# Output projection to up stage of a hybrid encoder layer: last row's scaling and third pair's weights ahead of casts, rows in two pools, four casts behind the block sums

## The chip, the cores and the metric

The kernel runs on one core of one Trainium2 chip. The metric is the time of one execution in device microseconds; the time of before is the median of three runs. The engines are TensorE (PE, with its weight loads PEld), VectorE (DVE), ScalarE (ACT), GpSimd (POOL) and SyncE (SP), which issues DMAs. Each takes its instructions in order, and they wait for each other through semaphores.

## The reference

One encoder layer over 1024 tokens (and 16 meta tokens) of width 1024. Cut to the part around the change:

```python
mix = jax.nn.sigmoid(gate_na) * y_na + jax.nn.sigmoid(gate_hg) * y_hg
h = h + mix @ w_o[l]                                   # output projection
m = rms_norm(h, norm_mlp[l])                           # each row scaled by rsqrt(mean(h*h) + eps), times a gain
h = h + jnp.square(jax.nn.relu(m @ w_up[l])) @ w_down[l]
```

Before it stand the input projection, a neighbourhood attention and a gated linear recurrence; behind it a final RMSNorm. All is float32.

## The kernel before

Every float32 matrix product is made of three matmuls: each operand is split into a rounded part (hi, cast by ScalarE) and the rest (lo, subtracted by VectorE), and hi*hi, hi*lo and lo*hi are added in PSUM. A split is thus one ScalarE cast and one VectorE subtraction of a 128x512 block.

**Output projection** (wo_rows). Eight rows of 128 tokens, two column halves each, 24 matmuls a half, into five PSUM banks in turn. VectorE adds each half into hres[i], into which SP has loaded that row of x. Then row_scale stores the row to DRAM (hsp[i], needed at the end of the layer), ScalarE squares it and sums, GpSimd makes the factor rs, and scale_row (VectorE) multiplies the row in place. TensorE transposes the scaled row in 128x128 blocks (turn_back), and row_sums makes the combinations of blocks that a Strassen-Winograd product needs: t1, t2, t3, t4 from b11, b21, b12, b22. Row j and row j+4 go together, so j runs from 0 to 3. split_rows casts one variant of one j into hi and lo tiles (nT, mT, nt1, nt3, nt4).

**Up stage.** w_up is worked off in 16 pairs of 128 columns. Each pair has seven products of 12 matmuls (chain, lines 918 to 920): product 1 with b11, 2 with b21, 3 with b22, 6 with t2, 5 with t1, 7 with t3, 4 with t4. Its weights are block sums (winograd, lines 908 to 911, four VectorE additions) and raw blocks, each split by weights (lines 1328 and 1329: tiles wh and wl). Pairs 0, 1 and 2 are early: their products 1 and 2 need no block sums, and run first, straight after the last row of the output projection, with weights loaded by first_load (tile sx). Then a loop takes pair 0's products 3, 6, 5, 7, and for the next pairs the rest, with the block sums of the next pair made by VectorE meanwhile.

**What sets the order.** From first_load(2) on, the order on TensorE, ScalarE, VectorE and GpSimd is as the code writes it (manual_schedule). The list todo holds the variants still to be cast: nine of j = 0 to 2 (t1, t3, t4), and five of j = 3. splits() takes the next ones; product_1 and product_2 call it between groups of three matmuls. Row 7 is finished in there: its square, its scaling (L1243), its transposes (L1268) inside pair 1's product 1, and row_sums(3) (VectorE L1249 and L1250, GpSimd L1251 and L1252).

**Memory.** The eight hres rows stand in one pool. When it closes, two loads of w_up for whole pairs (tile raw, L1355) and a second set of weight tiles (pool upr) take their place; each load waits for the last reader of the rows that it covers.

Of the kernel before, what the change touches and what calls it, by code (L numbers as in the profile page):

```python
# [9 lines left out]
F32 = mybir.dt.float32  # L10
F32R = mybir.dt.float32r
# [37 lines left out]
def layer(ctx: ExitStack, tc: tile.TileContext, x, meta, w_in, w_na, w_hg, w_o, w_up, w_dn,  # L49
# [1150 lines left out]
    hress = ExitStack()  # L1200
    hrp = hress.enter_context(tc.tile_pool(name="hrp", bufs=1, side="right", reuse_waits="tile"))
    hres = [None] * 8
    for i in (2, 6, 3, 7, 0, 4, 1, 5):
        hres[i] = hrp.tile([P, D], F32, name=f"hres{i}")
# [26 lines left out]
    def row_scale(i):  # L1231

        ssq = rowp.tile([P, 1], F32, tag="ssq", name="ssq", bufs=4)
        rs = rowp.tile([P, 1], F32, tag="rs", name="rs", bufs=4)
        tm = rowp.tile([P, 1], F32, tag="rtm", name="rtm", bufs=4)
        junk = rowp.tile([P, D], F32, tag="junk", name="junk", bufs=2)
        act.dma_start(hsp[i], hres[i])
        act.activation(junk, hres[i], AF.Square, accum_out=ssq)
        rsqrt_mean(rs, ssq, D, tm)
        return rs  # L1240
# [4 lines left out]
    def row_sums(j):  # L1245

        b11, b21, b12, b22 = (hres[i][:, q:q + TH] for i in (j, j + 4) for q in (0, TH))
        t2 = rowp.tile([P, TH], F32, tag="t2", name="t2", bufs=3)
        dve.tensor_tensor(b11, b12, b11, op=ALU.subtract)  # L1249
        dve.tensor_tensor(t2, b22, b11, op=ALU.subtract)  # L1250
        pool.tensor_tensor(b12, b22, b12, op=ALU.subtract)  # L1251
        pool.tensor_tensor(b21, b21, t2, op=ALU.subtract)  # L1252
        return {"t1": b11, "b22": b22, "t3": b12, "t2": t2, "t4": b21}
# [69 lines left out]
    def weights(src, pool_=None):  # L1323
        if pool_ is None:
            w_pools.append(w_pools.pop(0))
        hi, lo = (a_tile(pool_ or w_pools[-1], t, F32R, 1 if pool_ else 4) for t in ("wh", "wl"))
        v = (lambda t: t.rearrange("p (k c) -> p k c", c=P)) if len(src.shape) == 3 else (lambda t: t)
        act.copy(v(hi), src)  # L1328
        dve.tensor_tensor(v(lo), src, v(hi).bitcast(F32), op=ALU.subtract)  # L1329
        return hi, lo  # L1330
# [122 lines left out]
    def last_first_weights(k):  # L1453
        if k == 2:
            first_w[2].append(weights(first_raw[2][:, 4:], upf))

# [5 lines left out]
    with tc.manual_schedule(engines={e.engine for e in (pe, act, dve, pool, sp)}):  # L1462

        rs7 = row_scale(7)
        todo = [(v, j) for j in range(3) for v in ("t1", "t3", "t4")]
        todo += [(v, 3) for v in ("b22", "t2", "t1", "t3", "t4")]
# [5 lines left out]
        def last_row(k):  # L1472
            if k == 0:
                scale_row(7, rs7)
            elif k == 3:
                turn_back(hres[7][:, :TH], dve)
                turn_back(hres[7][:, TH:], act)
                nB.append(row_sums(3))
            else:
                splits()  # L1480

        product_1(pairs[0], first_w[0][0], lambda k: splits(k > 0))
        product_1(pairs[1], first_w[1][0], last_row)
        first_weights(2, 0)
        splits(2)
        product_1(pairs[2], first_w[2][0], lambda k: splits(), "mm")
        product_2(pairs[0], first_w[0][1], lambda k: (splits(k < 3), last_first_weights(k)))
# [4 lines left out]
        upr = ups.enter_context(tc.tile_pool(name="upr", bufs=1, side="right", reuse_waits="tile"))  # L1492
# [4 lines left out]
        next_weights(-1, "s4", "s2")  # L1497
        product_2(pairs[2], first_w[2][1])
# [3 lines left out]
        w_pools.insert(0, upr)  # L1502
        next_weights(-1, "s1", "s3", "a22")
        for m, q in enumerate(pairs):
# [3 lines left out]
            if m == 0:  # L1508
                product_6(q)
            if m + 1 < NP:  # L1510
                pair_sums(pairs[m + 1])
# [41 lines left out]
    ups.close()  # L1553
    up_s.close()
# [311 lines left out]
```

## Time and profile before

| | us |
|---|---|
| median of 3 runs | 1512.63 (1512.05 to 1513.26) |
| profiled execution | 1511.24 |
| its span, first to last instruction | 1509.5 |
| TensorE busy | 1492.1 |
| VectorE busy | 1035.8 |
| ScalarE busy | 665.0 |
| GpSimd busy | 370.7 |

The output projection runs from about 797 to 886 us of the span, products 1 and 2 of the early pairs from 885.7 to 907.4, the loop of the up stage to about 1197, and the down projection from there to the end. In rows of the trace the first number is the start in us from the start of the span, the second the duration; then come engine, line, operation, output and inputs, shapes, count, and in brackets the idle time before it and what ended that.

### The profile page before, as it was taken

To read this page: it belongs to the slowest core of one execution; us is meant where nothing else is said; L and a number is where in the kernel's file an instruction comes from. 1 tells how busy PE (TensorE), PEld (TensorE's weight loads), DVE (VectorE), ACT (ScalarE), POOL (GpSimd) and SP (SyncE) were. 2 spreads that over 40 slices of the span, in tenths; PEclk is the share of its full clock that TensorE was granted. 3 is DMA by queue.
4 is the path that set the end of the run, shared out by engine and by line. 5 is a ranking of instruction groups with operands and counts; after the bars stand their busy time and mean duration, and the time that the engine had idled before them with its cause. 6 is when DMAs were issued, how large, how long until landed. Compare 5 with 4: busy or idle time off the path is not lost.

```text
span 1509.5 us, 23492 instructions
## 1 busy us (share of the span) xinstructions
PE 1492.1 (99%) x9200; PEld 1250.8 (83%) x9200; DVE 1035.8 (69%) x1622; ACT 665.0 (44%) x1185; POOL 370.7 (25%) x349
## 2 busy tenths in 40 slices
PE   9999999999999999999999999999999999999998
PEld 8888888888888888888888878888888888888886
DVE  7876666656786796675585478777777445877876
ACT  7131313135565576343133355555555534334444
POOL 3313131324414400110000131344444200231242
PEclk9999999999999999999999999999999999999999
DMA  4211011114212237444655124544444676563224
GB/s 170 59 30 57 29 50 37 44 30 132 87 63 95 98 91 259 140 152 168 223 169 209 42 91 167 168 154 154 154 154 153 203 252 234 189 233 112 96 84 154
DMA packets 142592, 195.62 MB, mean 130 GB/s; under 512 B 8192, under 2 KB 90368, under 8 KB 142480
## 3 DMA queue, kind: packets, MB, share of 16 engines
q1 hardware_dynamic: 133072, 172.34, 34.8%
q10 hardware_dynamic: 7232, 14.44, 2.5%
q0 software_dynamic: 2176, 7.34, 1.3%
q8 instruction: 72, 1.18, 0.3%
q14 instruction: 40, 0.33, 0.1%
HBM read 139.56 MB, written 54.53 MB: 129 GB/s over the span
## 4 chain that ended last, share of the span: by engine, by line
PE 92%; DVE 4%; issue 2%; ACT 2%; POOL 0%; DMA 0%; POOLq 0%; ACTq 0%; DVEq 0%
PE mm L122 11%; PE mm L123 11%; PE mm L124 11%; PE mm L1541 5%; PE pa L1541 5%; PE pb L918 4%; PE pb L919 4%; PE pb L920 4%; PE pb L1541 4%; PE pc L1541 4%; PE pc L920 3%; PE pc L919 3%; PE pc L918 3%; PE pa L920 2%; PE pa L919 2%
## 5 line engine op out<-in xcount | busy, mean ns | idle before, releaser
L122 PE MATMUL mm<-aT,hi 128*128 128x512 f32 (+2 forms) x600 | 213.9, 357 | 0.0
L123 PE MATMUL mm<-aT,hi 128*128 128x512 f32 (+2 forms) x600 | 211.9, 353 | 0.0
L124 PE MATMUL mm<-aT,lo 128*128 128x512 f32 (+2 forms) x600 | 211.7, 353 | 0.0
L96 ACT CAST dh<-ur 128x1024 fp32r<-128x1024 f32 x54 | 56.9, 1054 | 166.5 <-issue 91.1
L97 DVE TENSOR_TENSOR dl<-ur,dh 128x1024 fp32r<-128x1024 f32 x54 | 70.0, 1297 | 87.0 <-ACT dh L96 85.2
L122 PEld LDWEIGHTS mm<-aT,hi 128*128 128x128 f32 x600 | 113.2, 189 | 12.6
L124 PEld LDWEIGHTS mm<-aT,lo 128*128 128x128 f32 x600 | 113.2, 189 | 12.3
L123 PEld LDWEIGHTS mm<-aT,hi 128*128 128x128 f32 x600 | 113.3, 189 | 12.0
L1333 ACT ACTIVATE uv<-uv 128x512 f32<-128x512 f32 x48 | 30.4, 633 | 82.3 <-DVE uv L1441 52.8
L1329 DVE TENSOR_TENSOR wl<-sx,wh 128x512 fp32r<-128x512 f32 x70 | 62.1, 897 | 3.6 <-ACT wh L1328 3.6
L1329 DVE TENSOR_TENSOR wl<-raw,wh 128x512 fp32r<-128x512 f32 x50 | 39.0, 783 | 36.4 <-ACT wh L1328 36.3
L112 ACT CAST hi<-raw 128x1024 fp32r<-128x1024 f32 x26 | 27.3, 1052 | 77.1 <-PE mm L123 71.3
L1328 ACT CAST wh<-sx 128x512 fp32r<-128x512 f32 x70 | 42.3, 620 | 38.5 <-PE pc L919 24.8
L1631 POOL TENSOR_TENSOR w<-w,tt 128x512 f32<-128x512 f32 x16 | 24.3, 1521 | 132.3 <-DVE tt L1630 111.1
L844 DVE CUSTOM_DVE_ANT_0 pr<-nsc,NB 128x432 f32<-128x432 f32 (+1 forms) x64 | 35.3, 560 | 30.2 <-issue 22.9
L300 POOL TENSOR_TENSOR Y<-X,TN 128x512 f32<-128x512 f32 x20 | 34.2, 1711 | 83.4 <-DVE X L297 83.4
L122 PE MATMUL mm<-wh,mT 128*128 128x512 f32 x128 | 50.2, 392 | 0.0
L123 PE MATMUL mm<-wl,mT 128*128 128x512 f32 x128 | 50.1, 391 | 0.0
L124 PE MATMUL mm<-o,lo 128*128 128x512 f32 x128 | 49.9, 390 | 0.1
L918 PE MATMUL pb<-nt,wh 128*128 128x512 f32 x128 | 49.9, 390 | 0.0
L124 PE MATMUL mm<-wh,mT 128*128 128x512 f32 x128 | 49.9, 390 | 0.0
L123 PE MATMUL mm<-o,hi 128*128 128x512 f32 x128 | 49.8, 389 | 0.0
(432 smaller groups left out, 4425.3 us busy)
## 6 DMA issues: line engine op xcount, KB each, us to landing
raw<-in_w_in SPq DMA_DIRECT2D x56, 512.0 KB, 3.9
ur<-usp SPq DMA_DIRECT2D x54, 512.0 KB, 3.6
raw<-in_w_up SPq DMA_DIRECT2D x16, 1024.0 KB, 6.2
usp<-us SPq DMA_DIRECT2D x60, 256.0 KB, 2.4
sg<-gsp SPq DMA_DIRECT2D x16, 512.0 KB, 5.1
w<-in_w_dn SPq DMA_DIRECT2D x16, 512.0 KB, 5.0
usp<-uv SPq DMA_DIRECT2D x30, 256.0 KB, 2.3
gsp<-gv ACTq DMA_DIRECT2D x24, 256.0 KB, 2.4
```

Source lines behind the costliest of these rows:

```text
L96: act.copy(hi, src)
L97: dve.tensor_tensor(lo, src, hi.bitcast(F32), op=ALU.subtract)
L122: pe.matmul(ps, lh, rh, start=first, stop=False)
L123: pe.matmul(ps, lh, rl, start=False, stop=False)
L124: pe.matmul(ps, ll, rh, start=False, stop=last)
L844: dve.tensor_tensor_reduce(out=pr[:, :w], in0=sc[:, :w], in1=NB[:, i, o:o + w], scale=1.0, scalar=3.0e38, op0=ALU.add, op1=ALU.min, accum_ ...
L918: pe.matmul(ps, lhs[0][:, c], rhs[0][:, k], start=first and k == 0, stop=False, skip_group_check=True)
L919: pe.matmul(ps, lhs[0][:, c], rhs[1][:, k], start=False, stop=False, skip_group_check=True)
L920: pe.matmul(ps, lhs[1][:, c], rhs[0][:, k], start=False, stop=k == 3, skip_group_check=True)
L1328: act.copy(v(hi), src)
L1329: dve.tensor_tensor(v(lo), src, v(hi).bitcast(F32), op=ALU.subtract)
L1541: pe.matmul(ps, a[n == 2][:, q, j * P:(j + 1) * P], b[n == 1][:, q], start=first and n == 0, stop=last and n == 2, skip_group_check=True)
```

## The change

Six edits, all in the stage above:

- the rows 2, 6, 3, 7 stand in a pool of their own (hrb), which stays open; when the other rows' pool closes, hrb's four slots hold the second set of weight tiles (hi and lo side by side), and pool upr goes;
- the store of row 7 (hsp 7) is issued on SP instead of ScalarE; the buffer for squares is one instead of two;
- the two subtractions of row_sums that GpSimd makes are made by VectorE for j = 3;
- the square and scaling of row 7 and the first half of the third pair's weights stand ahead of the casts, and those weights get two buffers of a pool of their own (upf);
- the second half of the third pair's weights stands ahead of product 1 of pair 2;
- t3 and t4 of j = 2 and 3 are cast later: two of them behind the casts of s4 and s2 for pair 0, one behind those of s1, s3 and a22, one behind pair 0's product 6.

```diff
+    hresb, hress = ExitStack(), ExitStack()
+    hrb = hresb.enter_context(tc.tile_pool(name="hrb", bufs=1, side="right", reuse_waits="tile"))
     hrp = hress.enter_context(tc.tile_pool(name="hrp", bufs=1, side="right", reuse_waits="tile"))
-    for i in (2, 6, 3, 7, 0, 4, 1, 5):
+    for i in (2, 6, 3, 7):
+        hres[i] = hrb.tile([P, D], F32, tag="hb", name=f"hres{i}", bufs=4)
+    for i in (0, 4, 1, 5):
         hres[i] = hrp.tile([P, D], F32, name=f"hres{i}")
...
-        junk = rowp.tile([P, D], F32, tag="junk", name="junk", bufs=2)
-        act.dma_start(hsp[i], hres[i])
+        junk = rowp.tile([P, D], F32, tag="junk", name="junk")
+        (sp if i == 7 else act).dma_start(hsp[i], hres[i])
...
-        pool.tensor_tensor(b12, b22, b12, op=ALU.subtract)
-        pool.tensor_tensor(b21, b21, t2, op=ALU.subtract)
+        eng = dve if j == 3 else pool
+        eng.tensor_tensor(b12, b22, b12, op=ALU.subtract)
+        eng.tensor_tensor(b21, b21, t2, op=ALU.subtract)
...
-        hi, lo = (a_tile(pool_ or w_pools[-1], t, F32R, 1 if pool_ else 4) for t in ("wh", "wl"))
+            pool_ = w_pools[-1]
+        if pool_ is hrb:
+            w = hrb.tile([P, D], F32R, tag="hb", name="wb", bufs=4)
+            hi, lo = w[:, :TH], w[:, TH:]
+        else:
+            hi, lo = (a_tile(pool_, t, F32R, 4 if pool_ is upw else 2) for t in ("wh", "wl"))
...
-        rs7 = row_scale(7)
-        todo = [(v, j) for j in range(3) for v in ("t1", "t3", "t4")]
-        todo += [(v, 3) for v in ("b22", "t2", "t1", "t3", "t4")]
+        todo = [(v, j) for j in range(2) for v in ("t1", "t3", "t4")] + [("t1", 2)]
+        todo += [(v, 3) for v in ("b22", "t2", "t1")] + [("t3", 2), ("t4", 2), ("t3", 3), ("t4", 3)]
...
         def last_row(k):
-            if k == 0:
-                scale_row(7, rs7)
-            elif k == 3:
+            if k == 3:
                 turn_back(hres[7][:, :TH], dve)
                 turn_back(hres[7][:, TH:], act)
-                nB.append(row_sums(3))
             else:
-                splits()
-
-        product_1(pairs[0], first_w[0][0], lambda k: splits(k > 0))
+                splits(k > 0)
+
+        def third_weights(q):
+            first_w.setdefault(2, []).append(weights(first_raw[2][:, 4 * q:4 * q + 4], upf))
+
+        splits()
+        rs7 = row_scale(7)
+        third_weights(0)
+        splits()
+        scale_row(7, rs7)
+        splits()
+        product_1(pairs[0], first_w[0][0])
         product_1(pairs[1], first_w[1][0], last_row)
-        first_weights(2, 0)
+        nB.append(row_sums(3))
         splits(2)
-        product_1(pairs[2], first_w[2][0], lambda k: splits(), "mm")
-        product_2(pairs[0], first_w[0][1], lambda k: (splits(k < 3), last_first_weights(k)))
+        third_weights(1)
+        product_1(pairs[2], first_w[2][0], lambda k: splits(k > 0), "mm")
+        product_2(pairs[0], first_w[0][1])
...
         product_2(pairs[1], first_w[1][1])
         next_weights(-1, "s4", "s2")
+        splits(2)
         product_2(pairs[2], first_w[2][1])
...
-        w_pools.insert(0, upr)
+        w_pools.insert(0, hrb)
         next_weights(-1, "s1", "s3", "a22")
+        splits()
...
             if m == 0:
                 product_6(q)
+                splits()
```

ScalarE's instructions from the casts of row 6's sums on. Names: hres7 is row 7, junk its square, ssq the sum, nt1, nt3 and nt4 are hi tiles of t1, t3 and t4, sx the third pair's raw weights, p1 a copy of product 1. Before:

```order
L1261 CAST mT10_8500<-t2_9195 128x4x128
L1237 DMA hsp7_8586<-hres7_8566 128x1024
L1238 ACTIVATE junk_9312,ssq_9309<-hres7_8566 128x1024
L1261 CAST nt10_9265<-hres0_8567 128x4x128
L1261 CAST nt30_9267<-hres4_8568 128x4x128
L1261 CAST nt40_9269<-hres0_8567 128x4x128
L1394 COPY p1_9317<-pa_9319 128x512
L1261 CAST nt10_9265<-hres1_8569 128x4x128
L1261 CAST nt30_9267<-hres5_8570 128x4x128
L1276 COPY hres7_8566<-pt_9362 128x512
L1394 COPY p1_9339<-pa_9341 128x512
L1328 CAST wh_9377<-sx_9305 128x512
```

The same place in the changed kernel:

```order
L1265 CAST mT10_8500<-t2_9198 128x4x128
L1265 CAST nt10_9268<-hres0_8570 128x4x128
L1241 ACTIVATE junk_9317,ssq_9314<-hres7_8569 128x1024
L1337 CAST wh_9322<-sx_9308 128x512
L1265 CAST nt30_9270<-hres4_8571 128x4x128
L1265 CAST nt40_9272<-hres0_8570 128x4x128
L1403 COPY p1_9331<-pa_9333 128x512
```

The store is gone from this queue, one cast stands ahead of the square, and the third pair's cast stands directly behind it, not behind pair 1's copy.

VectorE from the last sum of row 7 on. Names: rs is the row's factor, g2 the gain, nt11, nt31 and nt41 are lo tiles, pt the transposes, wl the lo part of weights. Before:

```order
L1216 TENSOR_TENSOR hres7_8566<-hres7_8566,mm_9230 128x512
L1262 TENSOR_TENSOR nt11_9266<-hres0_8567,nt10_9265 128x4x128
L1262 TENSOR_TENSOR nt31_9268<-hres4_8568,nt30_9267 128x4x128
L1262 TENSOR_TENSOR nt41_9270<-hres0_8567,nt40_9269 128x4x128
L1243 SCALAR_TENSOR_TENSOR hres7_8566<-hres7_8566,rs_9310,g2_8646 128x1024
L1262 TENSOR_TENSOR nt11_9266<-hres1_8569,nt10_9265 128x4x128
L1262 TENSOR_TENSOR nt31_9268<-hres5_8570,nt30_9267 128x4x128
L1276 COPY hres7_8566<-pt_9356 128x512
L1249 TENSOR_TENSOR hres3_8565<-hres7_8566,hres3_8565 128x512
L1250 TENSOR_TENSOR t2_9368<-hres7_8566,hres3_8565 128x512
L1329 TENSOR_TENSOR wl_9378<-sx_9305,wh_9377 128x512
```

The same place in the changed kernel:

```order
L1219 TENSOR_TENSOR hres7_8569<-hres7_8569,mm_9233 128x512
L1266 TENSOR_TENSOR nt11_9269<-hres0_8570,nt10_9268 128x4x128
L1338 TENSOR_TENSOR wl_9323<-sx_9308,wh_9322 128x512
L1266 TENSOR_TENSOR nt31_9271<-hres4_8571,nt30_9270 128x4x128
L1246 SCALAR_TENSOR_TENSOR hres7_8569<-hres7_8569,rs_9315,g2_8649 128x1024
L1266 TENSOR_TENSOR nt41_9273<-hres0_8570,nt40_9272 128x4x128
L1266 TENSOR_TENSOR nt11_9269<-hres1_8572,nt10_9268 128x4x128
L1266 TENSOR_TENSOR nt31_9271<-hres5_8573,nt30_9270 128x4x128
L1280 COPY hres7_8569<-pt_9363 128x512
L1252 TENSOR_TENSOR hres3_8568<-hres7_8569,hres3_8568 128x512
L1253 TENSOR_TENSOR t2_9379<-hres7_8569,hres3_8568 128x512
L1255 TENSOR_TENSOR hres7_8569<-hres7_8569 128x512
```

The third pair's wl came from behind the sums of row 3 to ahead of the scaling, nt41 of row 0 went behind it, and a subtraction that GpSimd made (L1255) stands on VectorE.

VectorE in the loop, from the weights of pair 0's product 5 to the first block sum of pair 1. Names: wb holds weights in a slot of hrb, uv is a sum of products 1 and 6, raw the pair's columns of w_up. Before:

```order
L1329 TENSOR_TENSOR wl_9506<-sx_9446,wh_9505 128x512
L1329 TENSOR_TENSOR wl_9510<-sx_9447,wh_9509 128x512
L1329 TENSOR_TENSOR wl_9514<-raw_9442,wh_9513 128x512
L1411 TENSOR_TENSOR uv_9536<-pb_9535,p1_9317 128x512
L908 TENSOR_TENSOR sx_9550<-raw_9444 128x512
```

The same place in the changed kernel:

```order
L1338 TENSOR_TENSOR wb_9501<-sx_9438,wb_9501 128x512
L1338 TENSOR_TENSOR wl_9505<-sx_9439,wh_9504 128x512
L1338 TENSOR_TENSOR wb_9508<-raw_9434,wb_9508 128x512
L1266 TENSOR_TENSOR nt31_9271<-hres7_8569,nt30_9270 128x4x128
L1420 TENSOR_TENSOR uv_9532<-pb_9531,p1_9331 128x512
L1266 TENSOR_TENSOR nt41_9273<-hres3_8568,nt40_9272 128x4x128
L908 TENSOR_TENSOR sx_9548<-raw_9436 128x512
```

One postponed cast stands ahead of the addition and one between it and the block sums.

More of the change, by code (lines that the diff above doesn't have):

```diff
@@ L1198, in layer @@
     mixs.close()
-    hress = ExitStack()
+    hresb, hress = ExitStack(), ExitStack()
+    hrb = hresb.enter_context(tc.tile_pool(name="hrb", bufs=1, side="right", reuse_waits="tile"))
     hrp = hress.enter_context(tc.tile_pool(name="hrp", bufs=1, side="right", reuse_waits="tile"))
     hres = [None] * 8
-    for i in (2, 6, 3, 7, 0, 4, 1, 5):
+    for i in (2, 6, 3, 7):
+        hres[i] = hrb.tile([P, D], F32, tag="hb", name=f"hres{i}", bufs=4)
+    for i in (0, 4, 1, 5):
         hres[i] = hrp.tile([P, D], F32, name=f"hres{i}")
@@ L1451, in layer @@
     upf = early_w.enter_context(tc.tile_pool(name="upf", bufs=1, reuse_waits="tile"))
-    def last_first_weights(k):
-        if k == 2:
-            first_w[2].append(weights(first_raw[2][:, 4:], upf))
     first_load(0)
@@ L1491, in layer @@
         rawp = ups.enter_context(tc.tile_pool(name="rawp", bufs=1, side="right", reuse_waits="tile"))
-        upr = ups.enter_context(tc.tile_pool(name="upr", bufs=1, side="right", reuse_waits="tile"))
         load_pair(0)
@@ L1553, in layer @@
     ups.close()
+    hresb.close()
     up_s.close()
```

## Prediction

> **What bounds the kernel now.** I read the page's busy shares, then a table of stretches around the changed stage, then what TensorE waits for there.
>
> ```profile
> PE 1492.1 (99%) x9200; PEld 1250.8 (83%) x9200; DVE 1035.8 (69%) x1622; ACT 665.0 (44%) x1185; POOL 370.7 (25%) x349
> ...
> 890.00:900.00 10.00, 6.29 (x30) 4.43 (x29) 9.86 (x12) 6.58 (x14) 3.48 (x2) 1.00 0.36 114
> ...
> PE mm L920 <- DVE wl L1329: 1.3, 1, 1.3
> PE pt L1268 <- DVE hres L1243: 1.2, 1, 1.2
> PE mm L918 <- ACT wh L1328: 1.2, 1, 1.2
> ```
>
> TensorE is busy 99% of the span, so only a wait of TensorE can be won. Between 780 and 960 us it has three, all in the stretch from 890 to 900, where it is busy 6.29 us of 10 and VectorE 9.86 (the columns are the stretch, its length, then PE, PEld, DVE, ACT and POOL, clock, DMA share, GB/s): it waits for the scaled last row, then for both halves of the third pair's weights. This stage holds no larger prize. The clock column says 1.00, so the waits cost no clock.
>
> ```profile
> 890.22 0.39 PE L920 MATMUL pa<-nT,wl 128*128 128x512 f32 x1
> 891.82 1.09 PE L1268 MATMUL pt<-ident,hres 128*128 128x128 f32 x8 [1.21 <-DVE hres L1243]
> 892.67 0.47 PE L918 MATMUL pa<-nT,wh 128*128 128x512 f32 x1
> ...
> 894.80 0.50 PE L918 MATMUL mm<-nT,wh 128*128 128x512 f32 x1 [1.19 <-ACT wh L1328]
> ...
> 896.83 0.50 PE L920 MATMUL mm<-nT,wl 128*128 128x512 f32 x1 [1.30 <-DVE wl L1329]
> ...
> 899.23 0.39 PE L918 MATMUL pa<-nT,wh 128*128 128x512 f32 x1
> ...
> 907.39 0.40 PE L918 MATMUL pc<-mT,wh 128*128 128x512 f32 x1
> ```
>
> A product is 12 matmuls; three of them fill 899.23 to 907.39, so a product without waits takes 2.72 us and a matmul 0.227. Starts, not modelled ends, are compared below.
>
> **Part 1: the third pair's weights (L1464 and L1328) move ahead.** From the matmul at 892.67 to product 3 of pair 0 at 907.39 pass 14.72 us. Work in it: three matmuls left of pair 1's product (0.31 for the first, which restarts, then 2 x 0.23, so 0.77) and four products (10.88), together 11.65. The two waits for weights with their restarts are therefore worth 14.72 - 11.65 = **3.07 us**. Afterwards the first half's weights are ready before 889.1 and needed after 892; the second half's, in the order shown above, at about 898 and needed at 900.6. Both waits go whole.
>
> **Part 2: the last row's scaling.**
>
> ```profile
> 885.89 0.69 DVE L1216 TENSOR_TENSOR hres<-hres,mm 128x512 f32<-128x512 f32 x1 [0.19 <-PE mm L124]
> 888.67 1.90 DVE L1262 TENSOR_TENSOR nt<-hres,nt 128x512 fp32r<-128x512 f32 x3 [2.10 <-ACT nt L1261]
> 890.48 1.28 DVE L1243 SCALAR_TENSOR_TENSOR hres<-hres,rs,g 128x1024 f32<-128x1024 f32 x1
> ...
> 892.88 0.69 DVE L1276 COPY hres<-pt 128x512 f32<-128x512 f32 x1
> ...
> 894.40 0.69 DVE L1250 TENSOR_TENSOR t<-hres,hres 128x512 f32<-128x512 f32 x1
> 895.01 1.77 DVE L1329 TENSOR_TENSOR wl<-sx,wh 128x512 fp32r<-128x512 f32 x1
> ...
> 886.98 1.06 ACT L1238 ACTIVATE junk<-hres 128x1024 f32<-128x1024 f32 x1 [4.01 <-DVE hres L1216]
> ...
> 888.03 1.65 ACT L1261 CAST nt<-hres 128x512 fp32r<-128x512 f32 x3
> ...
> 888.49 0.55 POOL L93 TENSOR_TENSOR rs<-rtm,half 128x1 f32<-128x1 f32 x1
> 894.44 1.79 POOL L1251 TENSOR_TENSOR hres<-hres 128x512 f32<-128x512 f32 x1 [5.40 <-DVE hres L1249]
> ```
>
> The scale rs is there at 889.04, but VectorE still has three subtractions of 0.60 us (start to start) queued ahead and scales at 890.48. The change leaves two ahead (wl, nt31); the third (nt11 of row 0) runs at 886.58, in a gap. ScalarE no longer issues the store of hsp 7, so its square starts at 886.61 instead of 886.98, and what follows is 0.37 us earlier: rs at 888.67, the next cast at 887.66 and its end, 0.62 later, at 888.28. VectorE: wl 888.30, nt31 888.90, scaling **889.50**. The scaling overwrites hres 7 and so also waits for the store, now issued on SP, where nothing stands ahead:
>
> ```profile
> 877.93 1.28 DVE L1243 SCALAR_TENSOR_TENSOR hres<-hres,rs,g 128x1024 f32<-128x1024 f32 x1 [2.73 <-DMA hsp<-hres]
> ...
> DMA to landing us min/median/max: 2.6/2.6/7.8
> ...
> hsp<-hres ACTq DMA_DIRECT2D x1, 512.0 KB, 7.8
> ```
>
> Row 6 was scaled 2.73 us after its sum, released by its store; the eight stores land in 2.6 us (median), and the 7.8 is row 0's, issued among eight loads. Row 7's sum ends at 886.58, so a quiet store allows 889.31; I take that, since all loads have landed by then, and keep 7.8 as the other end. Scaling to transposes is 1.34 us now (890.48 to 891.82): transposes at 890.84, that is **0.98 us** earlier. TensorE arrives at 890.45, so 0.4 us of wait stays.
>
> Gain up to product 3: 0.98 + 3.07 = **4.05 us**, so it would start at 903.34.
>
> **Part 3: are pair 0's block sums in time?** VectorE from the scaling: next instruction 1.20 us later (890.48 plus 1.20 and two casts of 0.60 is the copy's 892.88), at 890.70; three casts; copy at 892.50; the sums of row 3, spaced as from 892.88 to 895.01, end their two VectorE members with 894.63. The two subtractions that leave GpSimd follow (from 894.63 to 895.93, with a dependence). That costs little: GpSimd's at 894.44 made the wl at 895.01 last 1.77 instead of 0.69, so each took 1.1 us of VectorE anyway. Six casts more: block sums at 899.53, done in 2.6 us (913.88 to 917.18 below, less 0.66 for a cast), 902.14.
>
> ```profile
> 906.53 1.14 ACT L1328 CAST wh<-sx 128x512 fp32r<-128x512 f32 x2 [0.40 <-DVE sx L911]
> ...
> 910.82 0.58 ACT L1405 COPY uv<-pc 128x512 f32<-128x512 f32 x1
> 911.48 1.48 POOL L1406 TENSOR_TENSOR uv<-p,uv 128x512 f32<-128x512 f32 x1 [13.55 <-ACT uv L1405]
> ...
> 913.27 0.69 DVE L1411 TENSOR_TENSOR uv<-pb,p 128x512 f32<-128x512 f32 x1 [1.47 <-PE pb L920]
> 913.88 0.68 DVE L908 TENSOR_TENSOR sx<-raw 128x512 f32<-128x512 f32 x1
> 917.18 1.90 DVE L1329 TENSOR_TENSOR wl<-sx,wh 128x512 fp32r<-128x512 f32 x3 [0.69 <-ACT wh L1328]
> 920.19 0.68 DVE L1426 TENSOR_TENSOR uv<-uv,pb 128x512 f32<-128x512 f32 x1
> ...
> 918.96 0.39 PE L920 MATMUL pc<-mT,wl 128*128 128x512 f32 x1
> ...
> 921.23 0.39 PE L918 MATMUL pb<-nt,wh 128*128 128x512 f32 x1
> ...
> raw<-in_w_up SPq DMA_DIRECT2D x1, 1024.0 KB, 5.2
> ```
>
> ScalarE comes to the cast of s4, tied to pair 1's second product, at 906.53 - 4.05 = 902.48: 0.34 us of cover. The load of pair 0's rows waits on SP for nt41 of row 0 (ends 891.39) and lands 5.2 us later, 896.6, ahead of 899.53. SP's store of hsp 7 stands ahead of that load but issues at 886.6.
>
> **Part 4: what the four postponed casts give back.** Rows 2 and 3 of t3 and t4 are now cast in the loop. On ScalarE two casts (0.52 apart) stand ahead of s1's and a third ahead of the copy at 910.82, which thus comes at 910.82 - 4.05 + 1.56 = 908.33, and GpSimd's subtraction asks at 908.99. VectorE: s1, s3, a22 from 906.9, nt31 of row 3 until 909.39, then uv from pb (due 909.22) until 909.99. GpSimd's turn comes at 909.39; it holds VectorE's SBUF-only subtractions for 1.15 us to 910.54 (above, it asked at 894.44, came in when VectorE's 894.40 ended at 895.09, was done at 896.23, and the wl held behind it ended 0.55 later). The last cast, nt41 of row 3, held so, ends at 911.09, and pair 1's block sums start at 911.0, where 913.88 - 4.05 = 909.83 would have been: VectorE lags **1.17 us**. The uv addition at 920.19 (it frees pb for product 4) then ends at 920.87 - 4.05 + 1.17 = 917.99, product 4 starts at 918.04, its turn is 921.23 - 4.05 = 917.18. TensorE loses **0.86 us**, a little of it earlier, at the wl matmul (918.96 now). Later pairs have no postponed casts, and VectorE is then only 0.3 us behind.
>
> Whether uv, which reads one input from PSUM, is held too, no row of the trace shows:
>
> ```profile
> L1411 DVE TENSOR_TENSOR uv<-pb,p x16: 680/684/692, 913.3 to 1188.8; 128x512 f32<-128x512 f32 x16
> L911 DVE TENSOR_TENSOR sx<-raw,sx x24: 683/1772/1778, 579.5 to 1160.4; 128x512 f32<-128x512 f32 x24
> ```
>
> All 16 of L1411 are short, most of L911 long, but no L1411 starts inside a GpSimd subtraction. The ends are a lag of 0.67 (GpSimd slips past, no hold; 0.36 lost) and 1.77 (uv held too, 0.60 more; 1.46 lost); I take 1.17, nearest to the row, since no L1411 is long. [...]
>
> **Part 5: without cost.** The two pools swap addresses, so the loads of hres 0 and 1 wait for the last cast of mT:
>
> ```profile
> 796.88 4.90 DVE L97 TENSOR_TENSOR mT<-mix,mT 128x512 fp32r<-128x512 f32 x8
> 797.67 0.91 SPq L1206 DMA_DIRECT2D hres<-in_x  x2
> 805.63 1.29 DVE L1216 TENSOR_TENSOR hres<-hres,mm 128x512 f32<-128x512 f32 x2 [1.44 <-DMA hres<-in_x]
> ```
>
> They issue at 801.8 instead of 797.7, and row 0's sum comes about 4 us later; five PSUM banks of 5.4 us each (24 matmuls) cover that. Without this cover it would cost the 4 us. One junk buffer instead of two orders only ScalarE's own squares. In the loop a weight slot comes free one matmul (0.23 us) later; casts run microseconds ahead.
>
> **Sum.** 4.05 - 0.86 = 3.19 us: the profiled execution goes from 1511.24 (span 1509.5) to 1508.05. The median of the runs, 1512.63, lies 1.39 above it, so 1509.4.
>
> **Rivals.** (a) Forecast, lag as worked out, 3.19 (2.9 to 3.5): 0.45. (b) uv is held too: 4.05 - 1.46 = 2.6, 1510.0: 0.16. (c) The change doesn't do what it says for the row: ScalarE or VectorE is late by one more step and the scaling stays at 890.48, so 3.19 - 0.98 = 2.2, 1510.4; for it speaks that only two slots are gained: 0.14. (d) No hold, or slack that hides the lag: 3.7 to 4.05, 1508.6 to 1508.9: 0.17. (e) Slower: the store of hsp 7, alone on SP, takes long as row 0's did (7.8). The scaling starts at 894.5, 5.0 us after 889.50, and all behind it shifts: 1.8 us slower, 1514.4. It decides from a landing of 6.1 us (2.9 that cost nothing, plus 3.19), and passes 0.2% at 9.1; against it, no load is in flight then, and the median store takes 2.6: 0.08.
>
> 0.2% is 3.03 us, about what a measurement of this kernel can tell from no change; the forecast lies on that edge. Faster by more: 0.28 of (a) and all of (d), 0.45. Within: the rest of (a), 0.17, with (b), (c) and 0.03 of (e), 0.50. Slower by more: 0.05, the rest of (e), with what I overlook. The range goes from no loss at all with 0.2 of scatter, 1508.4, to a (c) with another microsecond of lag and the runs' spread of 0.6, 1511.8; (e) is left out.
>
> **What would show it.** After: TensorE's waits for wh and wl (L918, L920 on mm) are gone; transposes wait 0.4 us for the scaling; VectorE's scaling comes 2.9 us after the sum's end, 3.9 now; product 4 of pair 0 waits some 0.9 us for uv. Wrong if the scaling names the store as releaser, if s4's cast names the block sums with a long wait, or if TensorE waits again in pairs 1 and 2.

## The result and the profile after

| | before | after |
|---|---|---|
| median of 13 runs each, us | 1514.5 | 1510.26 |
| lowest and highest, us | 1512.05 to 1516.27 | 1508.92 to 1511.01 |
| profiled execution (its span), us | 1511.24 (1509.5) | 1510.21 (1508.4) |

The ratio is 0.9972, with a 95% interval from 0.9964 to 0.9981: 4.2 us faster (2.9 to 5.5), where 3.19 was forecast. The two profiled executions differ by only 1.03 us. That is no contradiction: in the profile of before, row 7's last sum on VectorE begins at 885.89 us, in that of after at 887.55, though the code up to there is the same. Executions of one program differ that much: two further profiles of the kernel before begin it at 887.01 and 886.49. So **all positions below are counted from the start of row 7's last sum**, the first point of the stage that the change doesn't move. By this count the stage was:

| us after the start of row 7's last sum | before | after | gained |
|---|---|---|---|
| VectorE scales row 7 | 4.59 | 3.74 | 0.85 |
| transposes of row 7 start on TensorE | 5.93 | 5.08 | 0.85 |
| first block sum of pair 0 | 17.92 | 13.69 | 4.23 |
| product 3 of pair 0 | 21.50 | 17.61 | 3.89 |
| product 4 of pair 0 | 35.34 | 32.31 | 3.03 |
| end of the span (listed to 0.1 us) | 623.61 | 620.85 | 2.76 |

The last row matters for the forecast, which was for the whole execution: 0.27 of the 3.03 us are given back behind the start of product 4. TensorE restarts there (its second matmul comes 0.35 us behind the first instead of 0.23), some 0.1 us more is lost by 65 us in this count, and from there to the end of the loop the two kernels keep the same distance.

First the page's busy shares after, then the same stretches (stretch, its length, then PE, PEld, DVE, ACT and POOL, granted clock, DMA share, GB/s):

```profile
PE 1493.8 (99%) x9200; PEld 1251.0 (83%) x9200; DVE 1036.5 (69%) x1624; ACT 664.7 (44%) x1185; POOL 366.3 (24%) x347
```

```profile
890.00:900.00 10.00, 9.64 (x48) 7.78 (x47) 9.85 (x15) 7.41 (x15) 0.38 (x1) 1.00 0.41 129
900.00:910.00 10.00, 10.00 (x45) 8.03 (x44) 7.63 (x14) 7.65 (x14) 0.00 (x0) 1.00 0.51 175
910.00:920.00 10.00, 9.58 (x42) 7.22 (x41) 9.24 (x15) 4.73 (x10) 1.56 (x1) 1.00 0.34 105
```

From 890 to 900 TensorE is now busy 9.64 us of 10 (6.29 before), with VectorE as full as it was. A new idle 0.42 stands from 910 to 920. TensorE's waits between 780 and 960 us, of the kernel after, name both:

```profile
PE pb L918 <- DVE uv L1435: 0.4, 1, 0.4
PE pt L1272 <- DVE hres L1246: 0.4, 1, 0.4
```

The waits for wh and wl are gone, that for the scaled row has shrunk from 1.2 to 0.4, and product 4 waits for uv. TensorE's rows, after:

```profile
892.63 1.09 PE L1272 MATMUL pt<-ident,hres 128*128 128x128 f32 x8 [0.36 <-DVE hres L1246]
...
894.26 0.40 PE L918 MATMUL mm<-nT,wh 128*128 128x512 f32 x1
...
905.16 0.40 PE L918 MATMUL pc<-mT,wh 128*128 128x512 f32 x1
...
919.86 0.51 PE L918 MATMUL pb<-nt,wb 128*128 128x512 f32 x1 [0.42 <-DVE uv L1435]
```

VectorE, after; the row 7 sum, the scaling with the two instructions ahead of it, then the loop's start:

```profile
887.55 0.69 DVE L1219 TENSOR_TENSOR hres<-hres,mm 128x512 f32<-128x512 f32 x1 [0.20 <-PE mm L124]
...
890.01 0.69 DVE L1338 TENSOR_TENSOR wl<-sx,wh 128x512 fp32r<-128x512 f32 x1 [1.17 <-ACT wh L1337]
890.62 0.69 DVE L1266 TENSOR_TENSOR nt<-hres,nt 128x512 fp32r<-128x512 f32 x1
891.29 1.28 DVE L1246 SCALAR_TENSOR_TENSOR hres<-hres,rs,g 128x1024 f32<-128x1024 f32 x1
...
901.24 0.68 DVE L908 TENSOR_TENSOR sx<-raw 128x512 f32<-128x512 f32 x1
...
911.11 0.68 DVE L1420 TENSOR_TENSOR uv<-pb,p 128x512 f32<-128x512 f32 x1
911.71 1.19 DVE L1266 TENSOR_TENSOR nt<-hres,nt 128x512 fp32r<-128x512 f32 x1
912.82 0.68 DVE L908 TENSOR_TENSOR sx<-raw 128x512 f32<-128x512 f32 x1
```

ScalarE's cast of s4 behind the block sums, which no longer names them:

```profile
904.30 1.14 ACT L1337 CAST wh<-sx 128x512 fp32r<-128x512 f32 x2 [0.40 <-ACT u L1343]
```

and GpSimd's one instruction of the time of the uv addition:

```profile
910.78 1.56 POOL L1415 TENSOR_TENSOR uv<-p,uv 128x512 f32<-128x512 f32 x1 [20.40 <-ACT uv L1414]
```

GpSimd runs from 910.78 to 912.34. The uv addition at 911.11, with one input in PSUM, starts and ends inside it and takes its ordinary 0.68; the cast behind it, with both inputs in SBUF, takes 1.19 instead of 0.69. This answers the open question of Part 4 at the place where it matters: uv is not held, nt41 is.

So the trace shows 3.03 us up to product 4 and 2.8 to the end, near the forecast of 3.19, and the medians show 4.2. The experiments ask two things: does each part do what the prediction says, and where does the rest, a microsecond or more, come from?

### The profile page after: what moved, and what is told of

Read it like the earlier page. It is cut to its first block, busy times and chain, and to the rows that moved or that the text cites. A ratio compares the mean times of both kernels' runs of the same rounds, so it can differ in the third digit from the quotient of the medians.

```text
span 1508.4 us, 23495 instructions
## 1 busy us (share of the span) xinstructions
PE 1493.8 (99%) x9200; PEld 1251.0 (83%) x9200; DVE 1036.5 (69%) x1624; ACT 664.7 (44%) x1185; POOL 366.3 (24%) x347
## 4 chain that ended last, share of the span: by engine, by line
PE 89%; DVE 5%; ACT 2%; issue 2%; DMA 2%; POOL 1%; ACTq 0%; POOLq 0%; DVEq 0%
PE mm L122 10%; PE mm L123 10%; PE mm L124 10%; PE mm L1554 5%; PE pa L1554 5%; PE pb L918 4%; PE pb L919 4%; PE pb L920 4%; PE pb L1554 4%; PE pc L1554 4%; PE pc L919 3%; PE pc L920 3%; PE pc L918 3%; PE pa L920 2%; PE pa L919 2%
## 5 line engine op out<-in xcount | busy, mean ns | idle before, releaser
L123 PE MATMUL mm<-o,hi 128*128 128x512 f32 x128 | 49.8, 389 | 0.0
L122 PE MATMUL mm<-o,hi 128*128 128x512 f32 x128 | 49.8, 389 | 0.0
L1554 PE MATMUL mm<-dl,dh 128*128 128x512 f32 x124 | 48.6, 392 | 0.3 <-DVE dl L97 0.2
L1554 PE MATMUL mm<-dh,dl 128*128 128x512 f32 x124 | 48.3, 389 | 0.0
L1554 PE MATMUL mm<-dh 128*128 128x512 f32 x124 | 48.1, 390 | 0.0
```

The costliest lines, as they stand in the source:

```text
L122: pe.matmul(ps, lh, rh, start=first, stop=False)
L123: pe.matmul(ps, lh, rl, start=False, stop=False)
L1554: pe.matmul(ps, a[n == 2][:, q, j * P:(j + 1) * P], b[n == 1][:, q], start=first and n == 0, stop=last and n == 2, skip_group_check=True)
```

## The experiments

Each ran beside the kernel before on the same chip; its median stands behind "against".

### Is the difference stable?

The changed kernel again, unedited.

> The changed kernel once more, beside runs of the kernel before on the same chip. All spans below are counted in the trace from the start of VectorE's last sum of row 7: to product 3 of pair 0 it was 21.50 us before and 17.61 after, to product 4 of pair 0 35.34 and 32.31. Theory A: the change's worth is what these spans show, 3.0 us, and the 4.2 us between the medians came from the kernel before, whose runs lay in two groups (1512.0 to 1513.3 and 1514.1 to 1516.3). Then the spans repeat within 0.1 and the medians differ by 2.5 to 3.5. Theory B: something outside this stage brings another 1.2 us; then the medians differ by about 4.2 again, with the same spans.

Measured: 1510.10 against 1513.97, ratio 0.9976 (0.9967 to 0.9985), 3.9 us. The positions repeat: scaling 3.75, product 3 at 17.64, product 4 at 32.34. So in the trace the stage is worth 3.0 us up to product 4 and 2.8 to the end again (620.86 us from row 7's last sum to the end of the span), while the medians have shown 4.2 and now 3.9. The interval (2.3 to 5.0 us) still holds A's 3.0, so this run alone decides nothing; whether there is another microsecond, and of what, stays open here.

### Part 1 alone

```
                 scale_row(7, rs7)
+                third_weights(0)
...
-        first_weights(2, 0)
         splits(2)
+        third_weights(1)
...
-        product_2(pairs[0], first_w[0][1], lambda k: (splits(k < 3), last_first_weights(k)))
+        product_2(pairs[0], first_w[0][1], lambda k: splits(k < 3))
```

(In the kernel before, with one junk buffer and two slots for the early weights, which make the room.)

> The kernel before with Part 1 alone: the third pair's weights ahead, all casts ahead of the block sums as before. Theory (the parts only pay together): the two waits of TensorE for wh and wl go, but VectorE has as much to do up to the block sums as before, so s4's sum ends where it ended (20.5 us after row 7's last sum began), ScalarE's cast of s4 now names it after a wait of some 2.5 us, and product 3 of pair 0 starts at 21.2 to 21.6 (before 21.50): 0 to 0.3 us gained. Rival (the waits for weights are the cost): product 3 at 18.4, 3.07 us gained.

Measured: product 3 at 21.27, product 4 at 35.27; 1515.05 against 1513.97, ratio 1.0007 (0.9998 to 1.0016). TensorE, then ScalarE, of this kernel:

```profile
907.95 0.50 PE L918 MATMUL pc<-mT,wh 128*128 128x512 f32 x1 [2.66 <-ACT wh L1328]
```

```profile
907.28 1.14 ACT L1328 CAST wh<-sx 128x512 fp32r<-128x512 f32 x2 [3.40 <-DVE sx L911]
```

The two waits for weights, 2.5 us together, come back as one of 2.66 at product 3: ScalarE can't cast s4 before VectorE's block sums, and these stand behind the same number of casts as before. The theory holds, and the rival (3.07 us won) falls. The 3.07 us of Part 1 are the price of these waits, but they are only collected together with the shorter queue ahead of the block sums. The median is no faster than before, though product 3 comes 0.23 earlier; in the profile the last store of the kernel takes 3.5 us from issue to landing, where it takes 2.7 before: 0.8 us against the 0.23 gained. Whether that holds for all its runs, and why, isn't shown.

### The four casts back ahead of the block sums

```
-        todo = [(v, j) for j in range(2) for v in ("t1", "t3", "t4")] + [("t1", 2)]
-        todo += [(v, 3) for v in ("b22", "t2", "t1")] + [("t3", 2), ("t4", 2), ("t3", 3), ("t4", 3)]
+        todo = [(v, j) for j in range(3) for v in ("t1", "t3", "t4")]
+        todo += [(v, 3) for v in ("b22", "t2", "t1", "t3", "t4")]
...
-        product_1(pairs[2], first_w[2][0], lambda k: splits(k > 0), "mm")
-        product_2(pairs[0], first_w[0][1])
+        product_1(pairs[2], first_w[2][0], lambda k: splits(), "mm")
+        product_2(pairs[0], first_w[0][1], lambda k: splits(k < 3))
```

(In the changed kernel; the calls that make the four casts in the loop go.)

> The changed kernel with the four postponed casts back ahead of the block sums. Theory (Parts 3 and 4): four casts of 0.60 us put the block sums 2.4 us later (first one 16.1 instead of 13.69 after row 7's last sum), s4's cast waits for them, product 3 of pair 0 starts at 19.6 instead of 17.61; the loss behind it is gone, so product 4 follows 13.85 us later as before, at 33.5 instead of 32.31: 1.2 us slower than the changed kernel. Rival 1 (the casts would have fitted in front, they bring only the lag): product 3 at 17.6, product 4 at 31.5, 0.9 faster. Rival 2 (the lag has another cause than these casts): product 3 at 19.6, product 4 14.7 later at 34.3, 2 us slower.

Measured: block sums at 16.09, product 3 at 19.41, as the theory has it, but product 4 at 35.04, which no theory had; 1511.69 against 1513.97. TensorE shows what came in between, and the stretches (columns as above) give it a name:

```profile
907.21 0.50 PE L918 MATMUL pc<-mT,wh 128*128 128x512 f32 x1 [1.62 <-ACT wh L1337]
...
908.99 0.63 PE L918 MATMUL pc<-mT,wh 128*128 128x512 f32 x1
909.42 0.63 PE L919 MATMUL pc<-mT,wh 128*128 128x512 f32 x1
...
911.12 0.63 PE L920 MATMUL pc<-mT,wl 128*128 128x512 f32 x1
```

```profile
900.00:910.00 10.00, 8.38 (x34) 6.29 (x33) 7.88 (x14) 6.37 (x12) 0.00 (x0) 0.95 0.48 164
910.00:920.00 10.00, 10.00 (x41) 8.13 (x40) 6.18 (x10) 3.35 (x7) 1.29 (x1) 0.88 0.37 120
```

From 908.99 on a matmul starts every 0.43 us instead of 0.23: **the granted clock has fallen to half**, 0.50 in each stretch of one us from 909 to 912. The clock column says for how long: 0.05 of ten us and 0.12 of ten us are missing, 1.7 us of full speed, which at half speed is 3.4 us. From product 3 to product 4 it took 15.63 instead of 13.85 us, 1.78 more. The casts themselves cost what Part 3 says. The second half of the expectation, that Part 4's loss is gone, is not tested by this run: TensorE has no wait at product 4, but the fall of the clock brought it there some 1.7 us later, so that a late VectorE could not have shown.

The wait ahead of it, 1.62 us, was shorter than the 2.66 us of the kernel with the weights ahead, whose clock stayed at 1.00. A wait of this size thus went with a lower clock in one execution and not in another. This pointed at the missing microsecond: the kernel before has 3.7 us of waits within 6.2 us, the changed one two of 0.4, 27 us apart. The runs list a mean clock each. Of the 82 runs of the kernel before beside all these experiments (one of 3630 us left out), 32 list 0.999, with a median of 1512.6 and 8 of them above 1513.5; 50 list 0.996 to 0.998, 43 of them above 1513.5. Of the changed kernel's 23, 21 list 0.999. The listing is a rough sign: it is rounded to 0.001, which is 1.5 us of full clock, and it counts the stretch behind TensorE's last matmul, where the column stands at 0.82 in the profile of before (1502.4 to 1509.5) and at 0.79 in that of after (1501.4 to 1508.4). The profile with the subtractions back on GpSimd (below) lists 0.998 without a fall in any stretch of 10 us up to 1500.

### The clock: more profiles of before, and filled waits

Two more profiles of the kernel before, unedited.

> The kernel before, for one more profile. With the casts back the clock column fell to half for 3.4 us after a single wait of TensorE of 1.6 us (0.95 and 0.88 in the two stretches behind it), where a wait of 2.7 us in the kernel with the weights ahead left it at 1.00. Theory C (the clock): the three waits of the kernel before, 3.7 us within 6.3, make the clock fall in some executions and not in others; those runs of it that list a clock of 0.997 or 0.998 (18 of 32) have a median of 1514.8 against 1513.1 for those at 0.999. Then a profile whose time is above 1514 shows matmuls of 0.43 us instead of 0.23 for 3.4 us behind a wait in the stretch from 890 to 900, and one below 1513.3 shows none there. Rival (the spread is from the transfers of earlier stages): a slow profile has a late start of row 7's last sum and no fall of the clock in this stretch.

> A further profile of the kernel before, as before_look1, which fell among the undisturbed ones (1512.4, clock 0.999, no fall in the stretch) and so did not tell. Theory C (the clock): above 1514 it shows matmuls of 0.43 us for 3.4 us behind one of the three waits; below 1513.3 none. Rival: a slow one without such matmuls there.

The first took 1512.42 us, with product 3 at 21.52 and product 4 at 35.34, and no fall. The second took 1513.50, with product 3 at 23.13 and product 4 at 36.97, 1.63 later. Its stretches from 890 to 910 and TensorE's rows:

```profile
890.00:900.00 10.00, 6.30 (x25) 4.38 (x24) 9.86 (x12) 6.61 (x13) 3.48 (x2) 0.88 0.33 106
900.00:910.00 10.00, 10.00 (x43) 8.00 (x42) 7.66 (x13) 6.37 (x12) 0.00 (x0) 0.95 0.49 159
```

```profile
897.44 0.73 PE L920 MATMUL mm<-nT,wl 128*128 128x512 f32 x1 [1.29 <-DVE wl L1329]
897.97 0.63 PE L918 MATMUL mm<-nT,wh 128*128 128x512 f32 x1
...
900.95 0.40 PE L919 MATMUL mm<-nT,wh 128*128 128x512 f32 x1
```

The same fall, 0.12 and 0.05, again 1.7 us, with 0.50 from 898 to 900, directly behind the third of the three waits. What the prediction's own profile did not have, this one has. Its time, 1513.50, lies between the two bounds that were set (above 1514 a fall, below 1513.3 none); the rival, a late start of row 7's last sum without a fall, does not describe it, since the sum starts early (886.49) and the clock falls.

Then the waits were filled: four matmuls into an unread bank in each.

```
+        def fill(n=4):
+            t = bank("a", "fill").rearrange("p a b -> p (a b)")
+            for j in range(n):
+                pe.matmul(t, first_w[0][1][0][:, :P], nV["b21"][0][:, j], start=True, stop=True)
```

> The kernel before with four matmuls of 0.23 us more in each of TensorE's three waits; their results go to a bank that nobody reads, and the waits for the data stay as they were. Theory C (the clock): the spans stay, product 3 of pair 0 at 21.5 and product 4 at 35.3 us after row 7's last sum, but the clock no longer falls: nearly all runs list 0.999, and the median comes down from 1514.0 to about 1513.1, 2.8 to 3.0 above the changed kernel. Rival (the second microsecond of the gain has nothing to do with the clock): the median stays at 1514.0, and 0.998 is listed as often as before.

Measured: 1513.18 against 1514.14 (1514.03 without the one run of 3630 us), 9 of 11 runs at 0.999, where 8 of 19 of before list it; product 3 at 21.52, product 4 at 35.34. Its waits, with what is left of them behind the fill:

```profile
893.96 1.09 PE L1270 MATMUL pt<-ident,hres 128*128 128x128 f32 x8 [0.30 <-DVE hres L1245]
...
896.94 0.50 PE L918 MATMUL mm<-nT,wh 128*128 128x512 f32 x1 [0.28 <-ACT wh L1330]
...
899.00 0.50 PE L922 MATMUL mm<-nT,wl 128*128 128x512 f32 x1 [0.40 <-DVE wl L1331]
```

Nothing arrives earlier, twelve matmuls are added, and the median falls by 0.85 us (0.96 with the odd run counted), as forecast from the clock. The ratio to before, 0.9997 (0.9988 to 1.0006), does not tell this from no change. A second estimate is that 50 of 82 runs, at 1.63 us for a fall, make 1.0 us on average. So one execution of the kernel before shows the fall and its price, and the listed clocks and the median agree with theory C; that the fall makes up the missing microsecond of the medians is not shown beyond their noise. Filled, the kernel before lies 3.0 us above the changed one's medians (1510.10 and 1510.26, which did not run beside it), near the 2.8 that the trace shows.

### Part 2 undone, whole and in part

The scaling where it was (the store on ScalarE, three casts ahead on VectorE, the third pair's first weights behind it), in the changed kernel:

```
-        (sp if i == 7 else act).dma_start(hsp[i], hres[i])
+        act.dma_start(hsp[i], hres[i])
...
-        splits()
         rs7 = row_scale(7)
-        third_weights(0)
-        splits()
-        scale_row(7, rs7)
-        splits()
+        splits(3)
```

(scale_row and third_weights(0) move into the between of pair 1's product 1.)

> The changed kernel with row 7's scaling where it was: its store on ScalarE again, three casts ahead of it on VectorE, the third pair's first weights behind it. Theory (Part 2): the scaling starts 3.9 us after the end of row 7's last sum instead of 3.05, the transposes wait 1.2 us instead of 0.4, and all behind them moves with it: product 3 at 18.5 and product 4 at 33.2, 0.85 to 0.98 us slower than the changed kernel. Rival (TensorE has slack further on, so the scaling's place does not matter): product 3 at 17.6 to 17.8, no slower.

And the store alone back on ScalarE, the first of these edits only:

> The changed kernel with the store of row 7 issued on ScalarE again, ahead of the square, as before; nothing else is changed. Theory (Part 2, first term): the issue holds ScalarE for 0.37 us, the square and the third pair's cast behind it come as much later, VectorE's wl waits for that cast, and the scaling starts 4.1 us after the start of row 7's last sum instead of 3.74; all behind it moves: product 3 of pair 0 at 18.0, product 4 at 32.7, 0.4 us slower than the changed kernel. Rival (the scaling is held by the store's landing or by VectorE's own queue, not by ScalarE): scaling at 3.74 to 3.8, product 3 at 17.6.

Measured, whole: scaling 4.59, product 3 at 18.45, product 4 at 33.15; 1511.30 against 1513.97. All is 0.84 later at product 3 and 4, as the scaling is: nothing further on absorbs it. Store alone: scaling 3.99, product 3 at 17.85, product 4 at 32.55; 1510.66 against 1514.73. It costs 0.25 at the scaling and 0.24 at the products, not 0.37. ScalarE's cast and VectorE's wl come 0.32 later, but in the changed kernel the scaling does not follow VectorE's row at once: it starts 0.67 behind nt31, not 0.60 as here. There the store, issued on SP at 888.27, landed 2.9 us later, at 891.17, just ahead of the scaling at 891.29. So the rival may be right for 0.07 us: store and queue end almost together. SP's row and the table of transfers of the changed kernel (its last column is us from issue to landing), then VectorE of the kernel with the store back:

```profile
888.27 0.33 SPq L1240 DMA_DIRECT2D hsp<-hres  x1
```

```profile
hsp<-hres SPq DMA_DIRECT2D x1, 512.0 KB, 2.9
```

```profile
890.63 0.68 DVE L1266 TENSOR_TENSOR nt<-hres,nt 128x512 fp32r<-128x512 f32 x1
891.23 1.28 DVE L1246 SCALAR_TENSOR_TENSOR hres<-hres,rs,g 128x1024 f32<-128x1024 f32 x1
```

### Part 3: the two subtractions back on GpSimd

```
-        eng = dve if j == 3 else pool
+        eng = pool
```

> The changed kernel with the two subtractions of row 3's sums back on GpSimd. Theory (Part 3: each takes VectorE 1.1 us either way, since GpSimd holds its two-input subtractions meanwhile): two subtractions in VectorE's row last about 1.77 instead of 0.69 and the block sums start within 0.6 us of where they start now (13.1 to 14.2 after row 7's last sum, now 13.69); product 3 at 17.6, product 4 at 32.3, no difference. Rival 1 (no hold, VectorE saves 1.3 us): block sums at 12.4 with all casts at 0.6 to 0.7. Rival 2 (it is needed for the sums to be in time): product 3 over 0.3 us later.

Measured: block sums at 14.67, product 3 at 17.99, product 4 at 32.87; 1511.73 against 1513.60. VectorE, GpSimd and ScalarE of this kernel:

```profile
897.19 3.49 DVE L1266 TENSOR_TENSOR nt<-hres,nt 128x512 fp32r<-128x512 f32 x2
```

```profile
896.62 1.81 POOL L1255 TENSOR_TENSOR hres<-hres 128x512 f32<-128x512 f32 x1 [5.44 <-DVE hres L1252]
898.39 1.75 POOL L1256 TENSOR_TENSOR hres<-hres,t 128x512 f32<-128x512 f32 x1
```

```profile
905.65 1.14 ACT L1337 CAST wh<-sx 128x512 fp32r<-128x512 f32 x2 [0.96 <-DVE sx L911]
```

Two casts that take 1.28 together undisturbed take 3.49: the hold is real, 2.2 us for the two, as Part 3 had it (1.1 each). But on VectorE the two subtractions take only 1.21, so on GpSimd they cost VectorE a net 1.0 us, and the block sums come 1.0 later. ScalarE's cast of s4 then waits for them (0.96 instead of 0.40 idle, and now for sx), and product 3 comes 0.38 later: rival 2 is right. Of the 1.5 to 1.6 us between the medians the stage shows 0.56 at product 4. In the profile, 0.8 us more lies at the other end of the kernel, where the last store takes 3.5 us to land instead of 2.7 (its line below); whether it does so in all runs, and why, isn't shown.

```profile
out<-hr ACTq DMA_DIRECT2D x1, 192.0 KB, 3.5
```

### Part 4: the lag in the loop

For pair 0, VectorE makes u3 straight from PSUM, ahead of s1's weights, which move behind product 3:

```
+        if q.m == 0:
+            dve.tensor_tensor(q.u3, q.p1, q.pc, op=ALU.subtract)
+        else:
             act.copy(q.u3, q.pc)
             pool.tensor_tensor(q.u3, q.p1, q.u3, op=ALU.subtract)
...
-        next_weights(-1, "s1", "s3", "a22")
-        splits()
...
             (product_3 if q.early else product_1)(q)
             if m == 0:
+                next_weights(-1, "s1", "s3", "a22")
+                splits()
```

> The changed kernel with pair 0's subtraction for u3 on VectorE, straight from the PSUM bank, placed ahead of the weights of s1 in a gap of 1.2 us; the copy on ScalarE and GpSimd's subtraction are gone for this pair. Theory (Part 4, the hold): the cast of nt41 of row 3, which lasted 1.19 behind GpSimd, takes 0.69, so pair 1's block sums start 0.5 us earlier (24.8 instead of 25.3 after row 7's last sum), the addition that frees pb ends as much earlier, and product 4 of pair 0 starts at 31.8 to 31.9 instead of 32.32. Rival (the two postponed casts alone make the lag, GpSimd nothing): product 4 at 32.3.

Measured: pair 1's block sums at 24.94, product 4 at 31.99; 1510.25 against 1514.14, ratio 0.9977 (0.9967 to 0.9987). The hold of 0.5 us is gone, but VectorE comes to the weights of s1 0.19 later than in the changed kernel (21.33 instead of 21.14), since the subtraction now stands ahead of them. So 0.32 us come back at product 4, not the expected 0.4 to 0.5; the rest of the lag stays. The median, 1510.25, is no lower than the changed kernel's. VectorE's rows show nt41 at its ordinary length:

```profile
911.07 0.69 DVE L1423 TENSOR_TENSOR uv<-pb,p 128x512 f32<-128x512 f32 x1
911.67 0.69 DVE L1266 TENSOR_TENSOR nt<-hres,nt 128x512 fp32r<-128x512 f32 x1
```

Then two casts were brought forward as well:

```
+        low = [cast(*todo.pop(0)) for _ in range(2)]
         product_2(pairs[1], first_w[1][1])
         next_weights(-1, "s4", "s2")
-        splits(2)
+        for f in low:
+            f()
```

> As u3_vector, and two of the four postponed casts go ahead on ScalarE of the squares of pair 1's product 2, where it waits 1.46 us, with their VectorE halves behind the weights of s4 and s2. Theory: everything behind them on ScalarE up to the weights of s1 is 1 us earlier, both last casts come ahead of the addition for u1, and VectorE is 1 us or more ahead of now: product 4 does not wait, and starts 13.9 us after product 3, at 31.5 to 31.6 (now 32.32): 0.8 us faster than the changed kernel, about 0.3 better than u3_vector. Rival (uv is not what holds product 4): no better than u3_vector. It misses if s4's cast comes later than now (16.75), for then product 3 moves back.

Measured: product 4 at 31.98, as without them; 1509.95 against 1514.14. A miss. VectorE of this kernel:

```profile
909.42 0.69 DVE L1415 TENSOR_TENSOR uv<-p,pc 128x512 f32<-128x512 f32 x1 [0.84 <-PE pc L920]
910.03 0.69 DVE L1338 TENSOR_TENSOR wb<-sx,wb 128x512 fp32r<-128x512 f32 x1
```

The subtraction put ahead of s1's weights waited 0.84 us for the end of product 3, and the earlier weights stood behind it in VectorE's row, at 910.03. With next_weights(-1, "s1") ahead of it:

> As both, with VectorE's half of the weights of s1 ahead of the subtraction for u3. In both that subtraction waited 0.84 us for the end of product 3 with s1's weights and all behind them queued after it, so the microsecond won on ScalarE went into this wait. Theory: the weights of s1 fill the wait, everything from s3 on is 0.6 us earlier on VectorE, the addition that frees pb is in time and product 4 of pair 0 starts in its turn, at 31.5 after row 7's last sum (both 31.98, changed kernel 32.32): 0.5 us faster than both. Rival (another link holds product 4): 31.9 to 32.0 again.

Measured: pair 1's block sums at 24.67, product 4 at 31.73, with no wait listed there; 1509.61 against 1513.60, ratio 0.9971 (0.9959 to 0.9982). Half of what was expected: 0.25 instead of 0.5 over both, so the weights of s1 were one link, and what holds the rest was not followed further. VectorE has now come so far forward that u1's addition waits 0.23 us for TensorE's pb. By the trace this is 0.58 us faster than the changed kernel and 3.6 faster than before; the intervals of the medians can't tell it from the changed kernel.

## Why the prediction was right, and where it was not

**Part 1** right in size, wrong alone: both waits of TensorE went, and 3.04 us with them (11.68 us from the restart at 893.48 to product 3, 14.72 before; 3.07 was forecast), but only because the postponed casts and the sums of row 3 on VectorE brought the block sums forward too. Alone, the same edit gives 0.23 us at product 3.

**Part 2** right, slightly oversized: 0.85 instead of 0.98 us, 0.4 of the wait left as said. 0.07 of the difference may be the store. Its landing was placed 2.73 us behind the sum's end, 0.19 ahead of the scaling; it took 2.9 us and landed just ahead of the scaling. The first term, 0.37 for the store's issue, measured 0.32 on ScalarE and 0.25 at the scaling. Rival (c), no gain here, fell; rival (e) fell too, though with less to spare than thought.

**Part 3** right: first block sum at 13.64 by the forecast, 13.69 measured, and s4's cast did not wait. But "costs little" for the two subtractions was the wrong conclusion from the right numbers: two holds of 1.1 against 1.21 of own work is a gain of 1.0, and without it the sums are late.

**Part 4** right, step by step. That GpSimd would not hold uv was taken from the short rows of L1411, none of which starts inside a GpSimd subtraction; the row at 911.11, with 0.68, shows it. The steps: VectorE's lag at pair 1's block sums was forecast as 1.17, and is 25.27 - (27.99 - 3.89) = 1.17. From product 3 to product 4 it took 14.70 instead of 13.84, 0.86 lost, the forecast number. Rivals (b) and (d) fell with the rows of uv and nt41 above. The wait of "some 0.9 us for uv" that was to show it is only half there: it is listed as 0.42, product 4 starts 0.58 behind its turn, and the other 0.28 are lost in the products ahead of it, 0.23 of that in the last one, whose matmuls start up to 0.34 us apart. What the sum left out is the restart behind product 4's start, 0.12 of the 0.27 us given back there.

**The sum**: 4.05 - 0.86 = 3.19 was forecast for the whole execution. The trace has 3.89 - 0.86 = 3.03 at product 4 and 2.8 at the end: 0.16 less up to product 3 (Parts 1 and 2), and 0.27 given back behind the start of product 4. **The step that failed** is the sentence ahead of the parts, "The clock column says 1.00, so the waits cost no clock". It was true of that execution. In another one (1513.50) the same three waits are followed by 3.4 us at half the clock, which cost 1.63 us. How often this happens is not measured; by the listed clocks it is worth about 1.0 us on average, which would make 3.8 of the trace's 2.8, inside both intervals of the medians (2.9 to 5.5 and 2.3 to 5.0). It also fits the spread of the runs, over 4 us before and 2.1 after: the start of row 7's last sum alone differs by 2.8 us between the profiles of all the kernels (885.89 to 888.70), and a fall adds 1.6.

**Luck.** The medians' 0.28% lies among the outcomes "faster by more than 0.2%", which were given 0.45, against 0.50 for "within". The trace's own 2.8 us, 0.18%, would have been within. So the side on which the result fell was not foreseen by the sum, and the clock, which the prediction had ruled out, is the likeliest reason for it.

**The absolute time**, 1510.26, came out 0.9 above the forecast of 1509.4, with a gain a full microsecond larger than forecast: the median of before, 1512.63 from three runs, rose to 1514.5 with thirteen, and the two errors went against each other. Carrying over the offset from the profile to the median, 1.39, did no harm: the profile of before was an early one (its last sum starts at 885.89, the mean of all 14 profiles is 887.4), and 1.39 is about what this is worth. By the trace, 0.4 of the 0.9 is the gain that was counted too high; the rest is no more than the scatter of the runs.

## What to carry to other kernels

Here a wait cost its length and, in two of the profiles, a fall of TensorE's granted clock to 0.50 behind it, which cost 1.63 and 1.78 us; the profile that the prediction read showed none of the second, so look at the spread of the runs and take a second profile before calling waits cheap. Compare a forecast for a whole execution with the trace up to its end, not only up to the last point of the stage. Where TensorE waited on one engine's full queue, taking away its two waits for weights, 2.5 us, moved them to the next instruction that this queue feeds, as one of 2.66, with 0.23 us gained; only with less work ahead of that instruction were 3.04 us collected. A two-input subtraction on GpSimd was not free for VectorE here: one of them cost VectorE 1.1 us, and doing it on VectorE 0.6.

## What the runs showed of the hardware

- **At this size of wait the granted clock fell in some executions and not in others.** Behind 1.62 us of idle in one stretch, and behind 1.2, 1.2 and 1.3 within 6.2 us, the granted clock went to 0.50 and 1.7 us of full clock were missing, 3.4 us at half, in one execution each; behind 2.66 us in one stretch in another kernel, and behind the same three waits in two other profiles, the column stayed at 1.00. What decides it is not shown.
- **Waits filled with useless matmuls** left 0.3 to 0.4 us of idle each, with no fall in the profile (matmuls 0.23 us apart behind them) and 9 of 11 runs at 0.999; the median came out 0.85 us lower without any data arriving earlier, which is within the noise.
- **GpSimd held one VectorE instruction and not the other**: inside one GpSimd subtraction of 1.56 us, a VectorE addition with one input in PSUM took its usual 0.68, and a cast's subtraction with both inputs in SBUF, which began in it, took 1.19 instead of 0.69. In the kernel with the subtractions back on GpSimd the same two took 0.68 and 1.19 beside one of 1.57.
